# The row loop of a PEER layer: dot, weighting and sum of a row at three places of the order, four row buffers of their own, and four projections as steps between rows

## The chip, the cores and the metric

One NeuronCore of a Trainium2 chip runs the whole layer in one launch. The metric is the device time in microseconds; the kernel before took 913.14 us (median of 3 runs, 912.76 to 917.01). TensorE is called PE here, VectorE DVE, ScalarE ACT, GpSimd POOL, and SyncE SP, which only issues DMAs.

## The reference, cut to what matters

A decoder layer on x of 256 positions by 1024, in float32: normalised projections, two attention groups, an output product with residual, then a PEER layer, in which each position picks 128 of 16384 experts and adds their weighted rows.

```python
h = rms_norm(x, attn_norm); P = h @ w_in            # 1024 x 3072: six parts of 512 columns
mq, mk, mv, dq, dk, dv = split(P)                   # MoBA q k v, differential q k v
...
x = x + concat(A, B) @ w_out
xc = rms_norm(x, ffn_norm)
q  = (xc @ w_query).reshape(C, 8, 2, 128)
sc = einsum('thpd,hpnd->thpn', q, sub_keys)         # 8 heads x 2 x 128 keys
top_s, top_i = top_k(sc, 16)
cand_s = top_s[:, :, 0, :, None] + top_s[:, :, 1, None, :]
best_s, best_pos = top_k(cand_s.reshape(C, 8, 256), 16)
experts = take_along_axis(cand_i, best_pos); gates = softmax(best_s)
u, vv = expert_down[experts], expert_up[experts]    # 128 experts a position, 1024 + 1024 values each
act = gelu(einsum('cd,chkd->chk', xc, u))
x = x + einsum('chk,chkd->cd', gates * act, vv)
```

The output has the shape of x. Every position reads 128 rows of 8 KB, so 256 x 128 x 8 KB = 268 MB come out of HBM.

## The kernel before, in words

The positions are two halves of 128, A and B (`tt` 0 and 1), one position to a partition. First half A runs alone: six projections (`proj`, `evac`, `turn`), attention, output product, norm, and the first of its four routes. `route(tt, c4)` finds the experts of two of the eight heads: `query` (64 matmul instructions of 128 columns on PE), `keys`, then `route1` and `route2`, a chain on DVE with products on POOL. Each route makes 32 expert numbers (`eid`, L556). Then the six projections of half B run, and only behind them does the row loop begin.

A **slot** is one expert for 128 positions. `issue` (L579) starts a gather of 128 rows of 8 KB into a row buffer `uv` (1.05 MB, L586, on POOL's queue) as soon as a buffer is free and its number is known. `slots` (L591) then emits for that row, one after the other: the dot product on DVE (L599), Gelu, times gate, and the diagonal `dg` on ACT (L600, L601, L603), and the sum on PE (L607, four matmul instructions of 512 columns into `acc`), and gives the buffer back. There are 256 slots, 128 for each half. Between slots the loop takes steps of a generator `behind`: one a slot, and one more every fifth (1.2 a slot). The steps are A's three other routes, then `front` (attention, output product, residual and norm of half B), then B's four routes; `yield` marks where a step ends.

Behind `tc.manual_schedule()` (L695) the instructions stand on every engine in the order in which this loop emits them; ahead of it a scheduler interleaves the work. Each engine takes its queue strictly in order, so an instruction that waits holds up all that stand behind it. There are 9 row buffers (`RING1`), made from the memory that the projections give back, and 6 more (`RING2`) when `front` has ended. Weights come in tiles of 512 KB on SP's queue: 20 buffers `wts` for projections and output product, 4 buffers `wqp` for the queries. PSUM has 8 banks: 4 `psA`, and 4 `psB` that later become two for `acc` and two for B's output product. `hdot` has 3 buffers, so a fourth dot waits until ACT has used the first.

```python
while done[0] < NT * NSEL:
    slots(1)
    next(work, None)
    if done[0] % 5 == 0:
        next(work, None)
    issue()
```

Of the kernel before, what the change touches and what calls it, by code (L numbers as in the profile page):

```python
# [20 lines left out]
P = 128  # L21
T = 256
NT = 2
# [20 lines left out]

RING1 = 9
RING2 = 6
WRING = 20


@with_exitstack  # L50
def hymba_peer_kernel(ctx, tc, xT_d, x_d, an_d, fn_d, fnT_d, win_d, qkg_d, lam_d, og_d, wout_d,
# [19 lines left out]
    pw = pj.enter_context(tc.tile_pool(name="pw", bufs=2, side="right"))  # L71
    qop = pj.enter_context(tc.tile_pool(name="qop", bufs=3, side="right"))

# [99 lines left out]
    def proj(ci, tt):  # L173
        p = pps[ci, tt] = psB.tile([P, 512], FT, name="psB")
        for k in range(KC):
            PE.matmul(p, lhsT=xT[tt][:, k], rhs=W[ci + 6 * tt][k // 2][:, k % 2], start=(k == 0), stop=(k == KC - 1))  # L176

    def evac(ci, tt):
# [8 lines left out]
        sq = aw.tile([P, 8, HD], FT, name="sq")  # L187
        S.activation(sq.rearrange("p h d -> p (h d)"), p, AF.Square, scale=r1[tt])
        ss = small.tile([P, 8], FT, name="ssq")
        V.tensor_reduce(ss, sq, axis=AX.X, op=OP.add)  # L190
        rs = small.tile([P, 8], FT, name="rsq")
        rsqrt(rs, ss, 8, HD)
        g0, n = GRP[ci]
        nh = 8 // n
# [3 lines left out]
        for m in range(n):  # L198
            for hf in range(2):
                a = slice(hf * 32, hf * 32 + 32)  # L200
                b = slice(32 - hf * 32, 64 - hf * 32)
                G.tensor_tensor(tv[:, :, m, a], prv[:, :, m, b],  # L202
                                ropeS[tt][:, None, g0 + m, a].to_broadcast([P, nh, 32]), op=OP.mult)
            V.tensor_tensor(ov[:, :, m], prv[:, :, m],
                            ropeC[tt][:, None, g0 + m, :].to_broadcast([P, nh, HD]), op=OP.mult)
        G.tensor_tensor(o, o, t, op=OP.add)
        V.tensor_tensor(o, o, bc(rs, HD), op=OP.mult)
        pend[ci, tt] = o
# [188 lines left out]
    sk = rt1.tile([P, 2 * PH, NKEY], FT, name="sk")  # L397
    proj(2, A)
    evac(2, A)
    proj(3, A)  # L400
    evac(3, A)
    turn(2, A)
    proj(0, A)
    evac(0, A)
    turn(3, A)
    run(scores(A, MOBA))
    proj(1, A)
    turn(0, A)
    evac(1, A)
    lambdas()  # L410
    run(probsT(A, MOBA))
    proj(5, A)
    evac(5, A)
    run(attend(A, MOBA))
    turn(1, A)
    run(scores(A, DIFF))
    run(mixturn(A, MOBA))
    proj(4, A)
    evac(4, A)
    for q in range(4):  # L420
# [167 lines left out]

    acc = {}

    def slots(n):  # L591
        for _ in range(n):
            if done[0] == NT * NSEL:
                return
            tt, k = divmod(done[0], NSEL)
            uv = rows.pop(done[0])
            col = cols[done[0]]
            h = small.tile([P, 1], FT, name="hdot")
            V.scalar_tensor_tensor(uv[:, :D], uv[:, :D], 1.0, xn[tt], op0=OP.mult, op1=OP.mult, accum_out=h)  # L599
            S.activation(h, h, AF.Gelu)  # L600
            S.activation(h, h, AF.Copy, scale=gate[tt][:, col:col + 1])  # L601
            dg = diag.tile([P, P], FT, name="dg")
            S.activation(dg, ident, AF.Copy, scale=h)  # L603
            if k == 0:
                acc[tt] = psO.tile([P, 2, 512], FT, name="acc")
            for c in range(2):
                PE.matmul(acc[tt][:, c], lhsT=dg, rhs=uv[:, D + c * 512:D + (c + 1) * 512],  # L607
                          start=(k == 0), stop=(k == NSEL - 1))
            rings.append(home.pop(done[0]))
            done[0] += 1  # L610
            issue()
            if k == NSEL - 1:
                for c in range(2):
                    m = slice(c * 512, (c + 1) * 512)
                    V.tensor_tensor(x2[tt][:, m], acc[tt][:, c], x2[tt][:, m], op=OP.add)  # L615
                    nc.sync.dma_start(out_d[tt * P:(tt + 1) * P, m], x2[tt][:, m])

    load_q(0, wts)
    run(route(A, 0))


    for g in (2, 3, 0, 1, 5, 4):
        fetch(g + 6, win_d[g], wts)
    gain_x(B, slice(0, 4))
    gain_x(B, slice(4, 8))
    norm_in(B)
    tables(B)
    for g in (2, 3, 0, 1, 5, 4):
        proj(g, B)
        evac(g, B)  # L630
        if g in (3, 1):
            turn(g - 1, B)
            turn(g, B)
    pj.close()
    wst.close()
    psP.close()
    psO = ctx.enter_context(tc.tile_pool(name="psO", bufs=1, space=PSUM))
    psW = right.enter_context(tc.tile_pool(name="psW", bufs=2, space=PSUM))
    bs = ExitStack()
    bp["b"] = bs.enter_context(tc.tile_pool(name="bp", bufs=1, side="right"))  # L640
    wqp = ctx.enter_context(tc.tile_pool(name="wqp", bufs=4))
    xb = ctx.enter_context(tc.tile_pool(name="xb", bufs=1))
    lists(B, xb)
    diag = ctx.enter_context(tc.tile_pool(name="diag", bufs=3))
    rings += [ctx.enter_context(tc.tile_pool(name="gat1", bufs=RING1))] * RING1

    def front():

        yield from both(B, MOBA)
        yield from both(B, DIFF)  # L650
        bs.close()
        wo2 = right.enter_context(tc.tile_pool(name="wo2", bufs=4, side="right"))
        for n in range(2):
            fetch(("o", n, B), wout_d[n], wo2, (0, 1))
        yield
        for n in range(2):
            for k in range(4):
                wout(B, n, k, psW)
                yield
        for n in range(2):  # L660
            fetch(("o", n, B), wout_d[n], wo2, (2, 3))
        yield
        for n in range(2):
            for k in range(4, 8):
                wout(B, n, k, psW)
                yield
        yield from resid(B, xb)
        yield from norm(B, xb)
        right.close()
        rings.extend([ctx.enter_context(tc.tile_pool(name="gat2", bufs=RING2, side="right"))] * RING2)  # L670

    def behind():
        f = front()
        yield from route(A, 1, 2)
        for n, _ in enumerate(route(A, 2, 3)):
            yield
            if n % 2:
                next(f, None)
                yield
        for _ in route(A, 3):  # L680
            yield
            next(f, None)
            yield
        yield from f
# [4 lines left out]

    load_q(1, wqp)  # L690
    ctx.enter_context(tc.manual_schedule())
    issue()
    work = behind()
    while done[0] < NT * NSEL:
# [61 lines left out]
```

## Time and profile before

| | |
|---|---|
| median of 3 runs | 913.14 us |
| profiled execution, its time | 912.12 us |
| profiled execution, its span | 910.2 us |
| busy share of the span: PE, DVE, ACT, POOL | 80%, 54%, 34%, 43% |
| DMA | 323.14 MB, mean 355 GB/s |
| gathers (256) | 268.85 MB, 73.6% of the 16 DMA engines' span |

The span runs from the first to the last instruction; 1.9 us of the profiled time lie outside it. Matmuls are pipelined and their ends are modelled, so the busy share of PE is too high a figure for its work. The 40 slices of the page are 22.76 us each. The first gather starts at 147 us, the last lands at 901 us.

### The profile page before, as it was taken

Reading aid. Unit: us, or ns where it says so; the run is one execution under the profiler, and the core shown is the slowest. Engines: PE = TensorE matmul, PEld = TensorE weight load, DVE = VectorE, ACT = ScalarE, POOL = GpSimd, SP = SyncE. Lnnn points to the kernel's source line nnn. Section 1 sums busy time; section 2 is a strip of 40 time slices with the busy share of each in tenths; the row PEclk is TensorE's granted clock in tenths of the full one; section 3 lists DMA queues with packets and bytes.
Section 4 is the critical chain, followed back from the end, with each engine's and each line's share of the span. In section 5 each row is a group of like instructions: output and inputs, shape, how many; then the busy total and the mean of one; then the engine's idle time right before and its main releaser. Section 6 shows DMA issues by size and latency. Waiting matters only on the chain. (4 is left out here: it accounts for less than half of the span.)

```text
span 910.2 us, 8337 instructions
## 1 busy us (share of the span) xinstructions
PE 729.8 (80%) x2156; PEld 340.9 (37%) x2156; DVE 491.0 (54%) x1364; ACT 311.1 (34%) x936; POOL 395.4 (43%) x426
## 2 busy tenths in 40 slices
PE   6998796788777787699885768686999787788876
PEld 2555342545335432344533435342343222222222
DVE  4744761373763576463574463646774444555443
ACT  1421112242552355332333232323443333333332
POOL 3400434272272254333555372728355555555540
PEclk9999988999899998999998999999899999999999
DMA  9997507999879788999999998978899999999995
GB/s 354 408 404 250 185 0 269 417 422 382 319 292 376 278 310 351 339 370 421 391 415 420 419 370 303 355 244 354 350 422 419 422 421 419 421 422 420 422 420 224
DMA packets 52686, 323.14 MB, mean 355 GB/s; under 512 B 6240, under 2 KB 6496, under 8 KB 19744
## 3 DMA queue, kind: packets, MB, share of 16 engines
q0 software_dynamic: 36944, 268.85, 73.6%
q1 hardware_dynamic: 15264, 53.12, 15.3%
q10 hardware_dynamic: 432, 0.66, 0.2%
q8 instruction: 17, 0.28, 0.1%
q14 instruction: 29, 0.24, 0.1%
HBM read 321.55 MB, written 1.05 MB: 354 GB/s over the span
## 5 line engine op out<-in xcount | busy, mean ns | idle before, releaser
L607 PE MATMUL acc<-uv,dg 128*128 128x512 f32 x1024 | 510.3, 633 | 158.2 <-ACT dg L603 157.6
L586 POOL DMA_INDIRECT uv<-in_uv_dram,eid x256 | 298.4, 1166 | 390.1 <-PE acc L607 203.2
L599 DVE SCALAR_TENSOR_TENSOR uv<-uv,xn 128x1024 f32<-128x1024 f32 x256 | 309.4, 1221 | 176.6 <-DMA uv<-in_uv_dram,eid 143.1
L607 PEld LDWEIGHTS acc<-uv,dg 128*128 128x128 f32 x1024 | 186.6, 196 | 441.9 <-ACT dg L603 278.4
L600 ACT ACTIVATE hdot<-hdot 128x1 f32<-128x1 f32 x256 | 51.0, 199 | 300.3 <-DVE uv L599 300.1
L603 ACT ACTIVATE dg<-ident,hdot 128x128 f32<-128x128 f32 x256 | 102.8, 401 | 55.3 <-PE acc L607 48.2
L176 PE MATMUL psB<-w,xT 128*128 128x512 f32 x192 | 91.2, 628 | 6.9 <-DMA w<-in_win_dram 6.9
L601 ACT ACTIVATE hdot<-hdot,gate 128x1 f32<-128x1 f32 x256 | 75.3, 294 | 8.3
L460 PEld LDWEIGHTS psA<-xgT,w 128*128 128x128 f32 x512 | 63.9, 198 | 14.5 <-issue 14.2
L460 PE MATMUL psA<-xgT,w 128*128 128x128 f32 x512 | 63.6, 280 | 0.0
L495 DVE MAX8 tops<-sc 128x8 f32<-128x128 f32 x32 | 7.0, 280 | 92.2 <-ACT sc L474 92.2
L483 POOL TENSOR_TENSOR ci<-tf 128x4 f32<-128x4 f32 (+3 forms) x72 | 32.5, 481 | 55.1 <-DVE tf L511 55.0
L176 PEld LDWEIGHTS psB<-w,xT 128*128 128x128 f32 x192 | 37.3, 201 | 49.9 <-issue 47.4
L555 DVE TENSOR_REDUCE ef<-hit 128x16 f32<-128x320 f32 (+1 forms) x16 | 11.7, 735 | 45.0 <-POOL hit L541 45.0
L338 PE MATMUL psB<-w,mT 128*128 128x512 f32 x64 | 30.5, 594 | 0.7 <-ACT mT L329 0.7
L202 POOL TENSOR_TENSOR qt<-pr,rS 128x128 f32<-128x128 f32 (+1 forms) x24 | 14.8, 640 | 30.4 <-ACT pr L186 30.3
L464 ACT COPY qs<-psA 128x512 f32<-128x512 f32 x8 | 4.7, 585 | 65.1 <-PE psA L460 65.1
L541 POOL TENSOR_TENSOR hit<-hit,ci 128x160 f32<-128x160 f32 (+1 forms) x32 | 23.4, 766 | 0.9 <-DVE hit L538 0.8
L599 DVE DVE_READ_ACCUMULATOR uv<-uv,xn 128x1 f32 x256 | 20.8, 81 | 0.0
L338 PEld LDWEIGHTS psB<-w,mT 128*128 128x128 f32 x64 | 11.8, 190 | 14.3 <-issue 13.4
L186 ACT ACTIVATE pr<-psB,r 128x512 f32<-128x512 f32 x8 | 5.5, 687 | 33.4 <-PE psB L176 22.2
L245 DVE TENSOR_REDUCE mx<-psA 128x2 f32<-128x512 f32 (+1 forms) x12 | 8.1, 685 | 14.3 <-PE psA L240 14.3
(125 smaller groups left out, 407.4 us busy)
## 6 DMA issues: line engine op xcount, KB each, us to landing
w<-in_win_dram SPq DMA_DIRECT2D x48, 512.0 KB, 9.5
w<-in_wq_dram SPq DMA_DIRECT2D x28, 512.0 KB, 9.6
w<-in_wout_dram SPq DMA_DIRECT2D x16, 512.0 KB, 10.0
uv<-in_uv_dram,eid POOLq DMA_INDIRECT x256, 12.1
sk<-in_sk_dram SPq DMA_DIRECT2D x1, 1024.0 KB, 9.7
out_dram<-x SPq DMA_DIRECT2D x4, 256.0 KB, 3.5
xT<-in_xT_dram SPq DMA_DIRECT2D x2, 256.0 KB, 5.0
x<-in_x_dram ACTq DMA_DIRECT2D x1, 512.0 KB, 6.1
```

What stands on the lines that cost most here:

```text
L176: PE.matmul(p, lhsT=xT[tt][:, k], rhs=W[ci + 6 * tt][k // 2][:, k % 2], start=(k == 0), stop=(k == KC - 1))
L202: G.tensor_tensor(tv[:, :, m, a], prv[:, :, m, b], ropeS[tt][:, None, g0 + m, a].to_broadcast([P, nh, 32]), op=OP.mult)
L338: PE.matmul(wops[tt, n], lhsT=mixT[tt, MOBA if k < 4 else DIFF][:, k % 4], rhs=W["o", n, tt][k // 2][:, k % 2], start=(k == 0), stop=(k == ...
L460: PE.matmul(p[:, c], lhsT=w[k // 2][:, k % 2, c * P:(c + 1) * P], rhs=xgT[tt][:, k], start=(k == 0), stop=(k == KC - 1))
L483: eng.tensor_tensor(d, src[:, :, 1, b0:b0 + nb], src[:, :, 0, a0:a0 + 1].to_broadcast([P, 2, nb]), op=OP.add)
L541: G.tensor_tensor(e[:, h], e[:, h], ci[:, h, None, :n].to_broadcast([P, 8, n]), op=OP.mult)
L586: G.indirect_dma_start(out=rows[n], out_offset=None, in_=uv_d, in_offset=bass.IndirectOffsetOnAxis(ap=eid[tt][:, k:k + 1], axis=0))
L599: V.scalar_tensor_tensor(uv[:, :D], uv[:, :D], 1.0, xn[tt], op0=OP.mult, op1=OP.mult, accum_out=h)
L600: S.activation(h, h, AF.Gelu)
L601: S.activation(h, h, AF.Copy, scale=gate[tt][:, col:col + 1])
L603: S.activation(dg, ident, AF.Copy, scale=h)
L607: PE.matmul(acc[tt][:, c], lhsT=dg, rhs=uv[:, D + c * 512:D + (c + 1) * 512], start=(k == 0), stop=(k == NSEL - 1))
```

## The change

The four parts:

- **Slot in three places.** `slots` becomes `dot`, `weigh` and `add`. In the loop the sum of a slot always follows one slot later than before; once B's projections have ended (`lag[0] = 1`) the weighting too follows one slot later, and the sum two. `hdot` gets 6 buffers. A buffer is given back, and the next gather issued, by `add`.
- **Four row buffers of their own.** `gat0` (`RING0` = 4) has its memory from the start, so that gathers need not wait for the projections' memory. `RING1` falls from 9 to 5 and joins when B's projections have ended; `RING2` is as it was. To make room `WRING` falls from 20 to 8, `qop` from 3 to 2; the `wqp` pool is there from the start.
- **Four projections as steps.** Of B's six projections only 2 and 3 run ahead of the slots. The others (0, 1, 5, 4) are steps at the head of `front`, four steps for the matmuls of each and up to five for its evacuation; their weights are fetched when each begins. B's projections and output product share two `psB` banks.
- **1.45 steps a slot** in place of 1.2, with `front` beginning earlier among A's routes.

```diff
-RING1 = 9
+RING0 = 4
+RING1 = 5
 RING2 = 6
-WRING = 20
+WRING = 8
+STEPS = 1.45
...
-    psP = ExitStack()
-    psB = psP.enter_context(tc.tile_pool(name="psB", bufs=4, space=PSUM))
+    psB = ctx.enter_context(tc.tile_pool(name="psB", bufs=2, space=PSUM))
+    psO = ctx.enter_context(tc.tile_pool(name="psO", bufs=1, space=PSUM))
+    wqp = ctx.enter_context(tc.tile_pool(name="wqp", bufs=4))
+    diag = ctx.enter_context(tc.tile_pool(name="diag", bufs=3))
+    gat0 = ctx.enter_context(tc.tile_pool(name="gat0", bufs=RING0))
...
             PE.matmul(p, lhsT=xT[tt][:, k], rhs=W[ci + 6 * tt][k // 2][:, k % 2], start=(k == 0), stop=(k == KC - 1))
+            if k % 2:
+                yield
...
+    acc, lag, dots, ready_w = {}, [0], [], []
+
+    def dot():
+        n = done[0]
+        done[0] += 1
+        h = small.tile([P, 1], FT, name="hdot", bufs=6)
+        uv = rows[n]
+        V.scalar_tensor_tensor(uv[:, :D], uv[:, :D], 1.0, xn[n // NSEL], op0=OP.mult, op1=OP.mult, accum_out=h)
+        dots.append((n, h))
+
+    def weigh():
+        n, h = dots.pop(0)
...
+        S.activation(dg, ident, AF.Copy, scale=h)
+        ready_w.append((n, dg))
+
+    def add():
+        n, dg = ready_w.pop(0)
...
+        rings.append(home.pop(n))
+        issue()
...
     def slots(n):
         for _ in range(n):
...
+            dot()
+            last = done[0] == NT * NSEL
+            while len(dots) > (0 if last else lag[0]):
+                weigh()
+            while len(ready_w) > (0 if last else 1):
+                add()
...
+    def project(g):
+        fetch(g + 6, win_d[g], wts)
+        yield from proj(g, B)
+        yield from evac(g, B)
...
+    run(project(2), project(3))
+    rings += [gat0] * RING0
...
     def front():
 
+        for g in (0, 1, 5, 4):
+            yield from project(g)
+        pj.close()
+        wst.close()
...
+        rings.extend([ctx.enter_context(tc.tile_pool(name="gat1", bufs=RING1))] * RING1)
+        lag[0] = 1
         yield from both(B, MOBA)
...
+        yield from mix(route(A, 1, 2), f, 2, 1)
+        yield from mix(route(A, 2, 3), f, 1, 1)
+        yield from mix(route(A, 3), f, 1, 1)
...
+        while steps < STEPS * (done[0] + 1):
             next(work, None)
-        if done[0] % 5 == 0:
-            next(work, None)
+            steps += 1
```

POOL around the first gathers, before: `hit` are the products of A's first route, `qt` and `qo` belong to B's projections, `uv` is a row buffer.

```order
L541 TENSOR_TENSOR hit_780<-hit_780,ci 128x400 x2
L206 TENSOR_TENSOR qo<-qo,qt 128x512
L202 TENSOR_TENSOR qt<-pr,rS_861 128x8x32 x2
L206 TENSOR_TENSOR qo<-qo,qt 128x512
L202 TENSOR_TENSOR qt<-pr,rS_861 128x4x32 x4
L206 TENSOR_TENSOR qo<-qo,qt 128x512
L202 TENSOR_TENSOR qt<-pr,rS_861 128x4x32 x4
L206 TENSOR_TENSOR qo<-qo,qt 128x512
L586 DMA uv<-in_uv_dram,eid_659 128x2048 x19
L483 TENSOR_TENSOR ci<-tf 128x2x8
```

The same place in the changed kernel, up to the products of A's second route (`ci`):

```order
L553 TENSOR_TENSOR hit_800<-hit_800,ci 128x400 x2
L217 TENSOR_TENSOR qo<-qo,qt 128x512
L598 DMA uv<-in_uv_dram,eid_671 128x2048
L212 TENSOR_TENSOR qt<-pr,rS_833 128x8x32 x2
L598 DMA uv<-in_uv_dram,eid_671 128x2048
L217 TENSOR_TENSOR qo<-qo,qt 128x512
L598 DMA uv<-in_uv_dram,eid_671 128x2048 x11
L495 TENSOR_TENSOR ci<-tf 128x2x8
```

The first gather now stands behind the evacuation of B's first projection; before it stood behind the last POOL work of all six.

SP from A's first query weights on, before (`wq` query weights, `win` projection weights, `wout` output product; 512 KB each):

```order
L83 DMA w<-in_wq_dram 128x1024 x4
L83 DMA w<-in_win_dram 128x1024 x24
L83 DMA w<-in_wq_dram 128x1024 x12
L83 DMA w<-in_wout_dram 128x1024 x8
L83 DMA w<-in_wq_dram 128x1024 x12
L616 DMA out_dram<-x_93 128x512 x2
```

And now, from the same point on:

```order
L88 DMA w<-in_wq_dram 128x1024 x4
L88 DMA w<-in_win_dram 128x1024 x8
L88 DMA w<-in_wq_dram 128x1024 x4
L88 DMA w<-in_win_dram 128x1024 x4
L88 DMA w<-in_wq_dram 128x1024 x4
L88 DMA w<-in_win_dram 128x1024 x4
L88 DMA w<-in_wq_dram 128x1024 x4
L88 DMA w<-in_win_dram 128x1024 x8
L88 DMA w<-in_wout_dram 128x1024 x8
L88 DMA w<-in_wq_dram 128x1024 x12
```

Of the 24 projection tiles 8 stand ahead of the second query's weights; the other 16 are now interleaved with the query weights of A's routes.

PE in B's third route, before, over the last quarter of its query (`psA_3242` is the query's bank, `qs_3241` its copy in SBUF, `dg_` the diagonals of successive slots):

```order
L607 MATMUL acc_1131<-uv_2988,dg_3281 128x512 x2
L460 MATMUL psA_3242<-xgT1_2628,w_3045 128x128 x2
L460 MATMUL psA_3242<-xgT1_2628,w_3047 128x128 x2
L460 MATMUL psA_3242<-xgT1_2628,w_3049 128x128 x2
L460 MATMUL psA_3242<-xgT1_2628,w_3051 128x128 x2
L607 MATMUL acc_1131<-uv_3006,dg_3300 128x512 x2
L473 MATMUL psA_3315<-sk_195,qs_3241 128x128 x4
L607 MATMUL acc_1131<-uv_3024,dg_3325 128x512 x2
```

ACT at that place, before:

```order
L603 ACTIVATE dg_3281<-ident_105,hdot_3277 128x128
L464 COPY qs_3241<-psA_3242 128x512
L600 ACTIVATE hdot_3296<-hdot_3296 128x1
L601 ACTIVATE hdot_3296<-hdot_3296,gate0_660 128x1
L603 ACTIVATE dg_3300<-ident_105,hdot_3296 128x128
```

PE there now (`psA_3148` and `qs_3147` are the query's bank and copy):

```order
L472 MATMUL psA_3148<-xgT1_2595,w_2971 128x128 x2
L472 MATMUL psA_3148<-xgT1_2595,w_2973 128x128 x2
L472 MATMUL psA_3148<-xgT1_2595,w_2975 128x128 x2
L472 MATMUL psA_3148<-xgT1_2595,w_2977 128x128 x2
L627 MATMUL acc_994<-uv_2877,dg_3179 128x512 x2
L485 MATMUL psA_3221<-sk_207,qs_3147 128x128 x4
L627 MATMUL acc_994<-uv_2897,dg_3206 128x512 x2
```

And ACT there now:

```order
L617 ACTIVATE dg_3179<-ident_117,hdot_3157 128x128
L476 COPY qs_3147<-psA_3148 128x512
L614 ACTIVATE hdot_3175<-hdot_3175 128x1
L615 ACTIVATE hdot_3175<-hdot_3175,gate0_672 128x1
L617 ACTIVATE dg_3206<-ident_117,hdot_3175 128x128
```

Before, the sum right behind the query used the diagonal that stands on ACT behind the copy of that query (`dg_3300`). Now it uses one that stands ahead of the copy (`dg_3179`), and the one behind it (`dg_3206`) is used a sum later.

## Rows read from the trace of the kernel before

**Rows 1.** The page's span in 40 slices: granted TensorE clock and DMA in tenths, and GB/s.

```profile
PEclk9999988999899998999998999999899999999999
DMA  9997507999879788999999998978899999999995
GB/s 354 408 404 250 185 0 269 417 422 382 319 292 376 278 310 351 339 370 421 391 415 420 419 370 303 355 244 354 350 422 419 422 421 419 421 422 420 422 420 224
```

**Rows 2.** Busy time by stretch for line L599 alone, the dot product; the count holds two instructions for each slot. Columns: stretch, its length, DVE busy (count), granted clock, DMA share, GB/s.

```profile
147.00:303.00 156.00, 51.73 (x86) 0.92 0.91 358
303.00:432.00 129.00, 49.32 (x83) 0.96 0.92 352
432.00:495.00 63.00, 21.79 (x39) 0.95 1.00 408
495.00:637.00 142.00, 45.83 (x77) 0.94 0.88 344
637.00:680.00 43.00, 32.43 (x53) 0.90 0.94 384
680.00:901.40 221.40, 108.75 (x179) 1.00 1.00 415
```

**Rows 3.** Who waited for whom from 147 to 660 us: us in total, times, longest.

```profile
POOL uv L586 <- PE acc L607: 197.4, 80, 7.4
...
PE acc L607 <- ACT dg L603: 115.4, 64, 9.1
...
DVE tops L495 <- ACT sc L474: 86.5, 7, 15.9
ACT qs L464 <- PE psA L460: 58.9, 7, 11.0
DVE ef L555 <- POOL hit L541: 43.2, 12, 8.7
DVE uv L599 <- DMA uv<-in_uv_dram,eid: 33.3, 10, 17.0
```

**Rows 4.** The timeline of B's second route, from its first query step to the first maximum of its scores: start, us, engine, line, count, and in brackets the idle time before and what ended it.

```profile
543.53 3.78 PE L607 MATMUL acc<-uv,dg 128*128 128x512 f32 x4 [4.70 <-ACT dg L603]
...
551.89 1.88 PE L607 MATMUL acc<-uv,dg 128*128 128x512 f32 x4
...
555.59 0.58 ACT L464 COPY qs<-psA 128x512 f32<-128x512 f32 x1 [10.97 <-PE psA L460]
...
556.64 0.40 ACT L603 ACTIVATE dg<-ident,hdot 128x128 f32<-128x128 f32 x1
557.09 1.98 PE L607 MATMUL acc<-uv,dg 128*128 128x512 f32 x4 [1.54 <-ACT dg L603]
...
560.72 0.87 DVE L495 MAX8 tops<-sc 128x8 f32<-128x128 f32 x4 [14.81 <-ACT sc L474]
```

**Rows 5.** The timeline of the start of the slots: A's first route from its first maximum to its expert numbers, the end of the second projection's evacuation on DVE, the first gather, the first dot and its way to PE.

```profile
95.49 0.87 DVE L495 MAX8 tops<-sc 128x8 f32<-128x128 f32 x4 [5.61 <-ACT sc L474]
...
110.18 0.17 DVE L556 CAST eid<-ef 128x32 int32<-128x32 f32 x1
...
117.92 0.17 DVE L125 SCALAR_TENSOR_TENSOR rsq<-rs_a,rsq 128x8 f32<-128x8 f32 x1
...
147.35 1.03 POOL L586 DMA_INDIRECT uv<-in_uv_dram,eid  x1 [13.31 <-PE psB L176]
...
153.23 1.23 DVE L599 SCALAR_TENSOR_TENSOR uv<-uv,xn 128x1024 f32<-128x1024 f32 x1 [16.96 <-DMA uv<-in_uv_dram,eid]
...
154.50 0.20 ACT L600 ACTIVATE hdot<-hdot 128x1 f32<-128x1 f32 x1 [5.99 <-DVE uv L599]
...
155.56 3.78 PE L607 MATMUL acc<-uv,dg 128*128 128x512 f32 x4 [9.08 <-ACT dg L603]
```

**Rows 6.** The 256 gathers of line L586, from issue to landing.

```profile
DMA to landing us min/median/max: 5.4/12.1/24.2
```

**Rows 7.** The page's DMA queues (packets, MB, share of the 16 engines' span) and issues (count, KB each, us to landing): the gathers' queue and one kind of weight tile.

```profile
q0 software_dynamic: 36944, 268.85, 73.6%
...
w<-in_wq_dram SPq DMA_DIRECT2D x28, 512.0 KB, 9.6
```

**Rows 8.** PE's timeline: one query, the keys of one route, and a run of 20 projection matmuls of 512 columns.

```profile
85.44 7.46 PE L460 MATMUL psA<-xgT,w 128*128 128x128 f32 x64
...
93.60 1.14 PE L473 MATMUL psA<-sk,qs 128*128 128x128 f32 x8
...
120.97 8.75 PE L176 MATMUL psB<-w,xT 128*128 128x512 f32 x20
```

**Rows 9.** Busy time in one stretch of the instructions that write or read `psA` (queries, keys, transposes, attention). Columns: stretch, its length, busy of PE, PEld, DVE and ACT (count), clock, DMA share, GB/s.

```profile
303.00:660.00 357.00, 51.21 (x384) 47.47 (x376) 4.82 (x7) 11.88 (x29) 0.94 0.92 358
```

**Rows 10.** The same stretch for line L338, B's output product: busy of PE and PEld.

```profile
303.00:660.00 357.00, 16.02 (x32) 6.08 (x32) 0.94 0.92 358
```

**Rows 11.** The chain of waits at its end: two links of gathers eight slots apart, and two pieces behind the last landing.

```profile
721.59 19.13 DMA uv<-in_uv_dram,eid
...
741.50 19.07 DMA uv<-in_uv_dram,eid
...
901.40 1.24 DVE uv L599 x2
...
905.70 0.69 DVE x L615
```

More of the change, by code (lines that the diff above doesn't have):

```diff
@@ L397, in hymba_peer_kernel @@
     sk = rt1.tile([P, 2 * PH, NKEY], FT, name="sk")
[L398 to L401, printed above, removed]
+    run(proj(2, A))
+    run(evac(2, A))
+    run(proj(3, A))
+    run(evac(3, A))
     turn(2, A)
-    proj(0, A)
-    evac(0, A)
+    run(proj(0, A))
+    run(evac(0, A))
     turn(3, A)
     run(scores(A, MOBA))
-    proj(1, A)
+    run(proj(1, A))
     turn(0, A)
-    evac(1, A)
+    run(evac(1, A))
     lambdas()
     run(probsT(A, MOBA))
-    proj(5, A)
-    evac(5, A)
+    run(proj(5, A))
+    run(evac(5, A))
     run(attend(A, MOBA))
@@ L417, in hymba_peer_kernel @@
     run(mixturn(A, MOBA))
-    proj(4, A)
-    evac(4, A)
+    run(proj(4, A))
+    run(evac(4, A))
     for q in range(4):
@@ L587, in issue @@
                                  in_offset=bass.IndirectOffsetOnAxis(ap=eid[tt][:, k:k + 1], axis=0))
-    acc = {}
+    acc, lag, dots, ready_w = {}, [0], [], []
[8 more added lines that the diff above has]
+        n, h = dots.pop(0)
+        col = cols[n]
+        S.activation(h, h, AF.Gelu)
+        S.activation(h, h, AF.Copy, scale=gate[n // NSEL][:, col:col + 1])
+        dg = diag.tile([P, P], FT, name="dg")
+        S.activation(dg, ident, AF.Copy, scale=h)
+        ready_w.append((n, dg))
@@ new lines, in add @@
+    def add():
+        n, dg = ready_w.pop(0)
+        tt, k = divmod(n, NSEL)
+        uv = rows.pop(n)
+        if k == 0:
+            acc[tt] = psO.tile([P, 2, 512], FT, name="acc")
+        for c in range(2):
+            PE.matmul(acc[tt][:, c], lhsT=dg, rhs=uv[:, D + c * 512:D + (c + 1) * 512],
+                      start=(k == 0), stop=(k == NSEL - 1))
+        rings.append(home.pop(n))
+        issue()
+        if k == NSEL - 1:
+            for c in range(2):
+                m = slice(c * 512, (c + 1) * 512)
+                V.tensor_tensor(x2[tt][:, m], acc[tt][:, c], x2[tt][:, m], op=OP.add)
+                nc.sync.dma_start(out_d[tt * P:(tt + 1) * P, m], x2[tt][:, m])
@@ L591, in slots @@
     def slots(n):
         for _ in range(n):
[L593 to L623, printed above, removed]
+            dot()
[4 more added lines that the diff above has]
+                add()
+    load_q(0, wqp)
+    run(route(A, 0, 1))
     gain_x(B, slice(0, 4))
@@ L627, in hymba_peer_kernel @@
     tables(B)
-    for g in (2, 3, 0, 1, 5, 4):
-        proj(g, B)
-        evac(g, B)
+    ORDER_B = (2, 3, 0, 1, 5, 4)
+    def project(g):
+        fetch(g + 6, win_d[g], wts)
+        yield from proj(g, B)
+        yield from evac(g, B)
         if g in (3, 1):
             turn(g - 1, B)
+            yield
             turn(g, B)
[L634 to L645, printed above, removed]
-    def front():
+            yield
+    run(project(2), project(3))
+    rings += [gat0] * RING0
+    lists(B, const)
+    xb = []
+    def front():
+        for g in (0, 1, 5, 4):
+            yield from project(g)
+        pj.close()
+        wst.close()
+        bs = ExitStack()
+        bp["b"] = bs.enter_context(tc.tile_pool(name="bp", bufs=1, side="right"))
+        xb = ctx.enter_context(tc.tile_pool(name="xb", bufs=1))
+        rings.extend([ctx.enter_context(tc.tile_pool(name="gat1", bufs=RING1))] * RING1)
+        lag[0] = 1
         yield from both(B, MOBA)
@@ L652, in front @@
         wo2 = right.enter_context(tc.tile_pool(name="wo2", bufs=4, side="right"))
[L653 to L665, printed above, removed]
+        for q in (0, 2):
+            for n in range(2):
+                fetch(("o", n, B), wout_d[n], wo2, (q, q + 1))
+            yield
+            for k in range(2 * q, 2 * q + 4):
+                for n in range(2):
+                    wout(B, n, k, psB)
                 yield
@@ L670, in front, with mix @@
         rings.extend([ctx.enter_context(tc.tile_pool(name="gat2", bufs=RING2, side="right"))] * RING2)
+    def mix(r, f, nr, nf):
+        n = 0
+        for _ in r:
+            yield
+            n += 1
+            if n % nr == 0:
+                for _ in range(nf):
+                    next(f, None)
+                    yield
     def behind():
         f = front()
[L674 to L683, printed above, removed]
+        yield from mix(route(A, 1, 2), f, 2, 1)
+        yield from mix(route(A, 2, 3), f, 1, 1)
+        yield from mix(route(A, 3), f, 1, 1)
         yield from f
@@ L693, in hymba_peer_kernel @@
     work = behind()
+    steps = 0
     while done[0] < NT * NSEL:
         slots(1)
-        next(work, None)
-        if done[0] % 5 == 0:
+        while steps < STEPS * (done[0] + 1):
             next(work, None)
+            steps += 1
         issue()
```

8 lines of the change are left out of this document (6 added, 2 removed).

## The prediction

> **What bounds the kernel now.** I read the page's 40 slices first [rows 1]. Three stretches show: up to slice 6 the DMA runs for weights only and falls to nothing; the middle, from 147 to about 680 us, is uneven; from slice 31 on every slice but the last moves 419 to 422 GB/s. That last stretch is bounded by the DMA: on the chain of waits two gathers eight slots apart start at 721.59 and 741.50 [rows 11], so a row of 1.05 MB takes 19.91 / 8 = 2.49 us. Nothing in the change moves fewer rows, so time can be won only where the DMA does not run at this rate.
>
> Then the stretches, by the count of dots [rows 2] (two instructions for each slot). The DMA's mean over 147 to 680 is (156 x 358 + 129 x 352 + 63 x 408 + 142 x 344 + 43 x 384) / 533 = 361 GB/s, 86% of 421. It idles there for about 75 us in sum, and before 147 it carries no row at all. A slot takes (303 - 153.2) / 43 = 3.49 us in the first 43 slots, and (637 - 303) / 99.5 = 3.36 us in the next hundred.
>
> Who is late there [rows 3]: POOL waits 197 us to issue gathers because PE has not given a buffer back, while DVE waits only 33 us for rows. Rows lie ready and slots are slow. PE in turn waits 115 us for the diagonal, DVE 87 us for the scores of a route, ACT 59 us for queries. The timeline of B's second route [rows 4] shows how: ACT waits 10.97 us for PE's query to copy it, the next diagonal stands behind that copy, PE waits 1.54 us for the diagonal, and DVE 14.81 us for the scores. No engine is full; strict order couples them.
>
> **The start.** The first gather goes out at 147.35, and POOL waited for PE's `psB` ahead of it, the last projections [rows 5]. Its expert numbers exist at 110.18 + 0.17. With `gat0` it needs these and POOL's first evacuation only: 110.4, 37 us sooner. The first dot stands on DVE behind the second projection's evacuation (117.92 + 0.17), and 110.4 plus the 5.88 us that the first row took (147.35 to 153.23) is 116.3, so it comes at 118.1 in place of 153.2: 35 us. Fewer weight buffers and two `psB` banks ahead of it I cost at nothing: PE's projection tiles take 8.75 / 20 x 4 = 1.75 us each [rows 8], a tile lands in 9.6 us at the median [rows 7], and 8 tiles of lead are 14 us of PE; without that cover each late tile would cost up to 8 us.
>
> **First stage, 43 slots on four buffers.** The steps from here to the end of B's projections are 1.45 a slot. Four projections are 4 x 16 x 0.44 = 28 us of PE; about three queries add 22.4 and keys 2.3 [rows 8]. Lower bounds for a slot:
> - the loop of a buffer: dot 1.23, ACT 1.06 (154.50 to 155.56), sum 1.88, issue to first dot 5.88 [rows 4, 5]; 10.05 / 4 = 2.51 us. The fastest landing of all is 5.4, the median 12.1 [rows 6], but the median belongs to a full queue of 9 to 15 rows.
> - PE: sum 1.75, plus 53 / 43 = 1.23: 2.98 us.
> - DMA: 2.49, plus 20 weight tiles at 1.25 us (half a row each), 25 / 43 = 0.58: 3.07 us.
>
> So no less than 3.07. With nothing hidden the buffer's loop pays for the rest: 2.51 + 1.23 + 0.58 + 0.87, the last being DVE's chain of a route (95.49 to 110.35, 14.9 us, 2.5 routes over 43 slots): 5.2 us. The row nearest to it is the first 43 slots of before at 3.49, with the same dots and routes and nine buffers. I add the projections and weight tiles that are new there, (28 + 25) / 43 = 1.23, at three tenths, as they lie beside other engines' work: 3.85 us. 43 slots end at 118.1 + 165.6 = 284, before 303.
>
> **Second stage, slots 43 to 128.** Now nine buffers, later fifteen, and weighting and sum lag. Lower bounds: DMA 2.49 + 20 tiles x 1.25 / 85 = 2.78; PE 1.75 + (51 + 16) / 85 = 2.54 [rows 9, 10]. Before it was 3.36, 0.87 above the DMA's 2.49. The steps are 1.45 / 1.2 = 1.21 times as dense, which alone gives 3.36 + 0.21 x 0.87 = 3.54. Against it stands the lag: PE's 115 us for the diagonal, over some 157 slots, are 0.73 a slot. In the order the sum behind a query now uses a diagonal that stands on ACT ahead of the query's copy, so that wait goes there; ACT's and DVE's own waits for the query (59 and 87 us) do not, and they are late next. Between none and all of 0.73 I take two fifths, 0.29: 3.25 us. 85 slots take 276: slot 128 at 560, with B's last route found by then (1.45 steps a slot bring it there some 20 slots earlier than before).
>
> **Last stage.** From there nothing but rows: some 13 have landed ahead, so 115 x 2.49 = 286 us remain: last landing 846. The tail, from the last landing's dot (901.40) past the last write at 905.70 to the span's end at 910.2, is 9 us; two dots in it, as now: 855. With 1.9 outside the span 857; the median of the runs shown is 1.0 above the profiled 912.12, so 858. As a check: 141 rows and 21 MB of weights, 169 MB from 113 to 560, are 379 GB/s, 90% of 421, against 86% before.
>
> Edits at nothing: three more `hdot` buffers, the same instructions in another order; the last slot sheds its lag at once. A sum that comes one or two slots later holds its buffer 3 to 6 us longer; with four buffers this stands in the 3.85, with fifteen it is covered by the rows ahead.
>
> **The clock.** The granted clock is 0.92 in 147 to 303 and 1.00 from 680 [rows 2]. After 9.08 us idle PE's first sum took 3.78 us, after 4.70 again 3.78, and 1.88 eight us later [rows 4, 5]: these are its two levels, 1.2 and 2.4 GHz. Four buffers leave PE idle more often.
> The Trainium skill, page "TensorE: Matmul & The Clock Gate", section "Part 1: The HAM clock gate (the "warmup" mystery)", says that half rate is the default state and that only sustained activity releases it. The rows agree with both levels, and it speaks against four buffers; by that rule alone, with PE at half rate throughout the first stage, the forecast would become the slower rival below.
>
> **The rivals.**
> - *The bubbles stay.* The lag moves a wait from PE to ACT and DVE, and the DMA stays at 361 GB/s: 169.1 MB / 0.361 = 468 us, slot 128 at 581, then 286 + 9 + 2 + 1: 879. For it: 87 us of DVE waiting for scores and 43 for `hit` [rows 3] are not touched. Against: the denser steps end sooner. It covers 868 to 905.
> - *The DMA is nearly full from the first gather.* At 97% of 421, 169.1 MB take 414 us: slot 128 at 527, the end at 825. The floor, all 290 MB at 421 from 113, is 689 + 113 + 11 = 813. For it: 0.73 us a slot of PE waits; against: the 3.07 of the first stage leaves no slack on four buffers.
> - *The gain is eaten.* Rows start 37 us sooner but the four buffers take 4.8 us a slot (43 slots: 206 us, 41 more than forecast): 858 + 41 and up, 899 to 917.
> - *Slower: four buffers and a slow PE.* A sum of 3.78 stands in the buffer's loop, and the loop becomes serial with PE's steps: (10.05 + 1.9) / 4 = 2.99 in place of 2.51, and queries and projections at half rate are 2 x 53 / 43 = 2.47 in place of 1.23; with 0.58 and 0.87 that is 6.9 if nothing overlaps, and 2 x 2.98 = 5.96 if PE alone decides. At 6.0 slot 43 comes at 376, 92 us later than forecast: 950. It decides from 3.85 + 56 / 43 = 5.15 us a slot on. For it: the 3.78 at the start, and PE, ACT and DVE waiting in turn even with nine buffers. Against: a clock of 0.92 with the same kind of waits, and four projections that give PE long runs of work.
>
> **How the numbers follow.** A measurement of this kernel can tell about 0.5% from no change: below 908.6 is faster, above 917.7 slower. Forecast 858 (its own range 835 to 868) 0.46; bubbles stay 0.24; DMA nearly full 0.11; gain eaten 0.08, of which a part ends within 0.5%; slower 0.11. Faster is then 0.46 + 0.24 + 0.11 + 0.01 = 0.82, the same 0.07, slower 0.11. The range leaves out at its low end half of the DMA-bound case, above it the last two: 826 to 908. The ends of the unknown costs give it too: 3.07 a slot in the first stage and 2.78 in the second would be 118 + 132 + 236 + 298 = 784, less than the floor, so 813 stands; 5.2 and 3.54 give 118 + 224 + 301 + 298 = 941.
>
> **What would show it.** First gather at 110 and first dot at 118. Slot 43 at 284, with 350 GB/s till then, slot 128 at 560, and 421 GB/s from there. PE's wait for the diagonal falls from 115 us to below half; the waits of DVE for scores stay. I am wrong if the first 43 slots take over 5.15 us each, with DVE waiting for rows and a clock well under 0.92, or if the diagonal's wait goes and the DMA still moves 361 GB/s up to slot 128.

## The result and the profile after

The changed kernel took 879.49 us (median of 4 runs, 873.64 to 882.52) against 912.95 us for the kernel before (4 runs, one more than above): ratio 0.962, 95% interval 0.956 to 0.968. The profiled execution took 878.93 us, its span 877.2 us. The prediction was 858, its range 826 to 908.

The page's 40 slices, now of 21.93 us each, with the rows that answer to [rows 1]:

```profile
PEclk9999969999999899988999999999999999999999
DMA  9969559989997999996999999999999999999993
GB/s 352 350 200 363 204 194 381 382 295 390 418 343 263 396 386 421 349 344 241 344 417 417 418 418 419 420 420 420 421 419 420 421 418 420 421 420 421 420 419 153
```

Counted from 1, rows now move from slice 6 on, and every slice from 21 (439 us) to 39 moves 417 GB/s and more, where before this began with slice 30 (660 us). In between lie four weak places: slices 6, 9, 12 to 13, and 17 to 20 with 241 GB/s at the bottom.

Busy time by stretch for the dots' line, L608, as in [rows 2]: stretch, its length, DVE busy (count, two instructions for each slot), granted clock, DMA share, GB/s.

```profile
113.00:284.00 171.00, 57.74 (x90) 0.95 0.89 339
284.00:395.00 111.00, 45.75 (x72) 0.92 0.97 379
395.00:425.00 30.00, 3.67 (x6) 0.89 0.72 247
425.00:560.00 135.00, 53.24 (x88) 0.96 1.01 415
560.00:581.00 21.00, 15.05 (x26) 0.92 1.01 421
581.00:868.00 287.00, 140.65 (x228) 1.00 0.99 411
```

Against 421 GB/s the DMA loses 171 x (1 - 339/421) = 33 us in the first stage, 11 in the next stretch, 12 in the 30 us behind 395, where only three dots run, and 2 in the 135 us up to 560: 59 us, most of it in the first stage, on four buffers.

Who waited for whom from 110 to 600 us, as in [rows 3]: us in total, times, longest.

```profile
POOL uv L598 <- PE acc L627: 181.5, 71, 10.9
...
DVE uv L608 <- DMA uv<-in_uv_dram,eid: 72.8, 43, 3.8
PE acc L627 <- ACT dg L617: 50.6, 33, 3.9
...
ACT qs L476 <- PE psA L472: 26.9, 6, 10.0
DVE x L358 <- PE psB L350: 26.0, 2, 25.8
DVE ef L567 <- POOL hit L553: 25.8, 9, 6.7
DVE tops L507 <- ACT sc L486: 25.0, 6, 12.7
```

Not only PE's wait for the diagonal has fallen (115 to 51); ACT's for a query (59 to 27) and DVE's for scores (87 to 25) fell with it. Two waits are new or larger: DVE for rows (33 to 73), and once 25.8 us for the output product.

The timeline of B's second route now, from its query's copy to the first maximum of its scores, the place of [rows 4]:

```profile
501.27 0.56 ACT L476 COPY qs<-psA 128x512 f32<-128x512 f32 x1
501.41 2.87 PE L627 MATMUL acc<-uv,dg 128*128 128x512 f32 x4 [2.02 <-ACT dg L617]
...
504.08 1.88 PE L485 MATMUL psA<-sk,qs 128*128 128x128 f32 x8
505.78 6.79 PE L627 MATMUL acc<-uv,dg 128*128 128x512 f32 x15
505.99 0.69 ACT L486 ACTIVATE sc<-psA,r 128x512 f32<-128x512 f32 x1 [3.29 <-PE psA L485]
...
506.71 0.87 DVE L507 MAX8 tops<-sc 128x8 f32<-128x128 f32 x4 [2.91 <-ACT sc L486]
```

Here the copy has waited for nothing (10.97 us before) and DVE 2.91 us for the scores (14.81 before); behind the keys PE runs at least 15 matmuls of sums in one piece, so their diagonals come in time. Other queries still wait: the 26.9 us of ACT above are six waits.

Starts of dots in the traces of this study (us; each the first instruction of that dot on DVE), used below:

```
dot            0      43     128    255
before         153.2  303.3  595.6  901.4
changed        118.7  279.2  563.6  868.3
e1 undone      118.4  284.7  650.9  946.0
e2 spread      155.8  288.1  539.2  849.8
e3 wout        118.6  281.7  549.6  854.6
e4 1.2 steps   117.5  276.0  543.8  864.2
e5 lag early   117.4  289.2  573.0  875.6
e6 five        119.5  270.4  552.3  857.3
e7 weigh       118.3  279.2  577.1  875.7
e8 wout+five   117.8  270.3  544.4  849.7
e9 sum         155.5  285.3  536.3  844.6
e10 1.2 undone 117.7  277.2  600.4  927.7
e11 copies     152.0  278.8  559.5  868.1
e12 wout+six   124.6  271.2  536.2  841.5
```

### The profile page after: what moved, and what is told of

Its sections match the earlier page's. It is cut to its first block, busy times and chain, and to the rows that moved or that the text cites. A ratio compares the mean times of both kernels' runs of the same rounds, so it can differ in the third digit from the quotient of the medians.

```text
span 877.2 us, 8338 instructions
## 1 busy us (share of the span) xinstructions
PE 725.2 (83%) x2156; PEld 337.4 (38%) x2156; DVE 497.9 (57%) x1364; ACT 311.8 (36%) x936; POOL 401.1 (46%) x426
## 4 chain that ended last, share of the span: by engine, by line
DMA 47%; PE 33%; DVE 9%; issue 5%; ACT 3%; POOL 2%; SPq 0%; DVEq 0%; POOLq 0%; ACTq 0%
DMA uv<-in_uv_dram,eid 43%; PE acc L627 14%; PE psB L181 7%; PE psA L472 4%; DVE uv L608 3%; DMA w<-in_wout_dram 3%; PE psB L350 3%; PE psA L252 1%; POOL hit L553 1%; PE psA L301 1%; POOL uv L598 1%; DMA w<-in_win_dram 1%; PE psA L485 1%; PE psA L251 1%; ACT dg L617 1%
## 5 line engine op out<-in xcount | busy, mean ns | idle before, releaser
L598 POOL DMA_INDIRECT uv<-in_uv_dram,eid x256 | 319.7, 1249 | 362.9 <-PE acc L627 182.6
L608 DVE SCALAR_TENSOR_TENSOR uv<-uv,xn 128x1024 f32<-128x1024 f32 x256 | 315.5, 1243 | 220.6 <-DMA uv<-in_uv_dram,eid 210.5
L627 PEld LDWEIGHTS acc<-uv,dg 128*128 128x128 f32 x1024 | 183.1, 194 | 395.5 <-ACT dg L617 235.5
L495 POOL TENSOR_TENSOR ci<-tf 128x4 f32<-128x4 f32 (+3 forms) x72 | 22.6, 344 | 56.8 <-DVE tf L523 56.7
L350 PE MATMUL psB<-w,mT 128*128 128x512 f32 x64 | 32.3, 640 | 8.3 <-DMA w<-in_wout_dram 7.6
L553 POOL TENSOR_TENSOR hit<-hit,ci 128x160 f32<-128x160 f32 (+1 forms) x32 | 25.8, 838 | 0.9 <-DVE hit L550 0.7
L358 DVE TENSOR_TENSOR x<-psB,x 128x512 f32<-128x512 f32 x4 | 2.8, 691 | 33.9 <-PE psB L350 33.9
L608 DVE DVE_READ_ACCUMULATOR uv<-uv,xn 128x1 f32 x256 | 21.4, 83 | 0.0
L226 PE MATMUL psA<-ident,qo 128*128 128x128 f32 x32 | 5.8, 311 | 12.4 <-DVE qo L219 12.4
```

Source lines behind the costliest of these rows:

```text
L350: PE.matmul(wops[tt, n], lhsT=mixT[tt, MOBA if k < 4 else DIFF][:, k % 4], rhs=W["o", n, tt][k // 2][:, k % 2], start=(k == 0), stop=(k == ...
L495: eng.tensor_tensor(d, src[:, :, 1, b0:b0 + nb], src[:, :, 0, a0:a0 + 1].to_broadcast([P, 2, nb]), op=OP.add)
L553: G.tensor_tensor(e[:, h], e[:, h], ci[:, h, None, :n].to_broadcast([P, 8, n]), op=OP.mult)
L598: G.indirect_dma_start(out=rows[n], out_offset=None, in_=uv_d, in_offset=bass.IndirectOffsetOnAxis(ap=eid[tt][:, k:k + 1], axis=0))
L608: V.scalar_tensor_tensor(uv[:, :D], uv[:, :D], 1.0, xn[n // NSEL], op0=OP.mult, op1=OP.mult, accum_out=h)
```

## The experiments

Theory 1 was the prediction's: the gain is the head start, the spread trims some idle time. Rival A: the spread carries the gain. Rival B: it costs, by holding buffers.

**e1, the spread undone.** In the changed kernel:

```diff
-            while len(ready_w) > (0 if last else 1):
+            while len(ready_w) > 0:
...
-        lag[0] = 1
```

> The changed kernel with dot, weighting and sum of a slot in one place again, rest as changed. Theory 1 (the gain is the head start of 35 us; the spread only trims the idle time of the DMA in the row loop, which is about 65 us in the changed kernel against 73 before): 5 to 12 us slower than the changed kernel, 884 to 892 us, with PE's wait for the diagonal back from 51 to 80 us or more between 110 and 600 us. Rival A (the spread carries the gain: without it four buffers take over 5 us a slot): 905 us or more. Rival B (the spread holds each of the four buffers a slot longer and costs time in the first stage): 876 us or less, and slot 43 before 270 us.

965.45 us, ratio to before 1.058 (1.052 to 1.065): 86 us slower than the changed kernel and slower than before. Theory 1 falls. But A's condition does not hold either: the first 43 slots took (284.7 - 118.4) / 43 = 3.87 us, not over 5. The loss lies behind them, (650.9 - 284.7) / 85 = 4.31 us a slot (its trace is of a run of 956.74 us, the shortest of its four). Its waits from 284 to 660 us show the same set as before:

```profile
POOL uv L598 <- PE acc L627: 179.6, 54, 8.5
...
PE acc L627 <- ACT dg L617: 90.5, 51, 6.4
DVE tops L507 <- ACT sc L486: 64.9, 5, 14.9
...
ACT qs L476 <- PE psA L472: 50.5, 5, 10.8
```

**e2, the spread alone.** The kernel before with `dot`, `weigh`, `add` called by `slots`, `lag[0] = 1` from the start, and six `hdot` buffers as in the changed kernel:

```diff
-    acc = {}
+    acc, lag, dots, ready_w = {}, [1], [], []
...
+        h = small.tile([P, 1], FT, name="hdot", bufs=6)
...
+            dot()
+            last = done[0] == NT * NSEL
+            while len(dots) > (0 if last else lag[0]):
+                weigh()
+            while len(ready_w) > (0 if last else 1):
+                add()
```

> The kernel before with the spread slot alone (weighting one slot later and sum two, from the first slot on; 9 buffers, all six projections ahead). Theory 1: 5 to 10 us faster than before, 903 to 908 us; PE's wait for the diagonal under 60 us where it was 115. Rival A: 895 us or less. Rival B: 913 us or more.

856.54 us, ratio 0.935 (0.929 to 0.942). Rival A holds: the spread alone wins 55 us, though its first gather leaves at 150. The rest of the change, put on top, costs 23 us.

**e3, the output product as before.** The changed kernel with the loops of the kernel before: the two column halves `n` one after the other, and a `yield` behind each `wout`. The changed kernel has `n` inside and one `yield` for both halves of a `k`.

```diff
-            for k in range(2 * q, 2 * q + 4):
-                for n in range(2):
-                    wout(B, n, k, psB)
+        for n in range(2):
+            for k in range(4):
+                wout(B, n, k, psB)
+                yield
...
```

> The changed kernel with the output product of half B in 18 steps as in the kernel before, in place of 4. Theory 1: the hole of the DMA at 395 to 425 us (247 GB/s, 12 us lost) comes of the four dense steps, in which DVE's residual stands ahead of the dots while PE waits for weight tiles: without it 867 to 873 us, and DVE's wait for that product falls from 26 us to below 10. Rival: the step count decides, 14 more steps put B's routes 10 slots later and give the gain back: 876 to 884 us.

866.71 us, ratio 0.950 (0.945 to 0.955): 13 us, at the low edge of what was expected. The product takes 10 steps in the changed kernel, not the 4 that the text above says: two that fetch, and eight with one `k` of both halves; e3 makes them 18. DVE's wait:

```profile
DVE x L358 <- PE psB L350: 6.7, 1, 6.7
```

The changed kernel's timeline shows what the denser steps did: PE waits for a weight tile of the second half, and DVE, whose residual is emitted behind the last of these steps, 25.84 us for PE; all later dots stand behind it.

```profile
404.22 2.08 PE L350 MATMUL psB<-w,mT 128*128 128x512 f32 x2 [5.35 <-DMA w<-in_wout_dram]
...
416.07 0.69 DVE L358 TENSOR_TENSOR x<-psB,x 128x512 f32<-128x512 f32 x1 [25.84 <-PE psB L350]
```

In e3 PE waits for no tile of this product. Step count and loop order were changed together; which of them won the 13 us is not shown.

**e4, 1.2 steps a slot** (`STEPS = 1.2`).

> The changed kernel at 1.2 steps a slot. Theory 1: B's last route ends some 25 slots later, the DMA reaches its 420 GB/s later, but each slot on the way is faster: 884 to 892 us. Rival (idle time goes by the step, not by the slot): 877 to 882 us, the same. Rival (dense steps overload the slots with four buffers): 872 us or less.

880.41 us, ratio 0.964 (0.959 to 0.969): the same as the changed kernel; the rival holds. With the spread in, the density of the steps is worth nothing: dot 128 comes 20 us sooner, and the 127 slots behind it take 16 us longer (320 against 305).

Theory 2: four buffers pace the first stage. Rival C: weights and PE do.

**e5, the weighting's lag from the first slot on.**

```diff
-    acc, lag, dots, ready_w = {}, [0], [], []
+    acc, lag, dots, ready_w = {}, [1], [], []
```

> The changed kernel with the weighting one slot late and the sum two from the first slot on, not from the end of half B's projections. Theory 2 (four buffers pace the first stage: about 15 us from one dot on a buffer to the next, 11 of them from issue to dot, 3.73 us a slot; a later sum lengthens that loop by a slot): slot 43 at 310 to 325 us where it was at 279, the whole 890 to 905 us. Rival A (the spread pays wherever it stands, as in the spread alone, 3.08 us a slot in the first 43 slots): slot 43 at 255 to 270 us, the whole 858 to 870 us.

887.7 us, ratio 0.976 (0.972 to 0.980), 8 us slower, slot 43 at 289. The sign is theory 2's, the size below what it said (slot 43 is 10 us later, not 31 to 46): both values lie between the two stated ranges.

**e6, five own buffers.**

```diff
-RING0 = 4
-RING1 = 5
+RING0 = 5
+RING1 = 4
...
-WRING = 8
+WRING = 6
```

> The changed kernel with five row buffers of their own and four that join in place of 4 and 5, and 6 weight buffers in place of 8 to make the room. Theory 2: a loop of 15 us over five buffers is 3.0 to 3.2 us a slot, slot 43 at 250 to 260 us, and the whole 858 to 866 us, if the first stage's 20 us are kept to the end. Rival C (late weights and PE's steps pace the first stage, not the buffers; two weight buffers fewer make that worse): slot 43 at 278 us or later, 878 us or more.

867.48 us, ratio 0.953 (0.949 to 0.957), 12 us faster. The whole came 1.5 us and slot 43 (270) 10 us later than theory 2 allowed: 3.51 us a slot in place of 3.73. DVE's wait for rows up to slot 43, in the changed kernel (113 to 284 us) and here (113 to 270):

```profile
DVE uv L608 <- DMA uv<-in_uv_dram,eid: 55.2, 31, 3.8
```

```profile
DVE uv L608 <- DMA uv<-in_uv_dram,eid: 35.3, 23, 3.7
```

So buffers are a part of what paces this stage, by 0.22 us a slot, not all of it.

**e7, the weighting never late.**

```diff
-        lag[0] = 1
```

> The changed kernel with the sum one slot late throughout and the weighting never late: one of the two halves of the spread undone. If the weighting's lag carries the 86 us that the spread is worth in the changed kernel (ACT does it ahead of the copy of a query it would stand behind): 930 to 955 us, PE's wait for the diagonal between 284 and 585 us over 60 us where it is 23. If the sum's lag carries it: 880 to 895 us. If each gives its share: 900 to 925 us.

883.95 us, ratio 0.971 (0.966 to 0.976): some 4 of the 86 us, within what a repeat differs by. PE's wait for the diagonal between 284 and 585 us is 36 us, not over 60 (23 in the changed kernel). In the changed kernel the sum's single slot carries the spread.

**e8, output product as before and five own buffers** (the edits of e3 and e6).

> Two edits in one: five own buffers (and 6 weight buffers) and the output product of half B in 18 steps. Theory 2: the two holes are apart in time, so the gains add: 12 of the output product and 15 to 20 of the buffers, 844 to 853 us, below the spread alone (856.5). Rival (what one gives back the other takes, since the DMA cannot be moved past its 420 GB/s: both end at the same bound): 860 to 868 us.

854.68 us, ratio 0.937 (0.931 to 0.943). The gains add (13 + 12 = 25); the upper end of the range was missed by 2 us, and the time is level with e2, not below it.

Theory 3: the sum's slot works because PE no longer stands at a diagonal that ACT makes behind the copy of PE's own query. Rivals D to F stand in the texts.

**e9, the sum's lag alone.** e2 with `lag = [0]`: on the kernel before, the sum one slot late, and the six `hdot` buffers of e2, which the text does not name.

> The kernel before with the sum one slot late throughout and nothing else (weighting at once, 1.2 steps, 9 buffers). Theory 3 (the sum's one slot carries nearly all of the spread, because PE no longer stands at a diagonal that ACT makes behind the copy of the query PE has just ended): 856 to 866 us, against 856.5 for the whole spread alone and 912 for before; PE's wait for the diagonal between 150 and 600 us at 60 us or less where it was 103. Rival D (with nine buffers and the projections ahead it takes both lags): 875 to 895 us.

855.39 us, ratio 0.935 (0.931 to 0.939), the same as e2 and half a microsecond below theory 3's range. The waits of the kernel before from 150 to 600 us:

```profile
POOL uv L586 <- PE acc L607: 180.6, 74, 7.4
...
PE acc L607 <- ACT dg L603: 103.2, 57, 9.1
...
DVE tops L495 <- ACT sc L474: 77.9, 6, 15.9
ACT qs L464 <- PE psA L460: 52.6, 6, 11.0
...
DVE uv L599 <- ACT dg L603: 20.1, 9, 5.1
```

And in e9, whose routes end sooner, from 150 to 550 us:

```profile
POOL uv L586 <- PE acc L615: 129.6, 68, 5.8
...
DVE tops L495 <- ACT sc L474: 53.2, 7, 10.3
...
PE acc L615 <- ACT dg L605: 52.1, 32, 13.8
...
ACT qs L464 <- PE psA L460: 33.9, 6, 7.5
...
DVE uv L596 <- ACT dg L605: 3.7, 2, 2.4
```

PE's wait for the diagonal up to 600 us is 58.4, within the 60 that were expected. The last row is dots that wait until ACT frees an `hdot` buffer: 20.1 us before, 3.7 here. What six buffers alone are worth was not run; e1 has six and no lag, and is slower than before. The clock does not explain the gain: the granted clock from 284 to 560 us was 0.95 before and is 0.96 in e9.

Its GB/s in 40 slices, of 21.3 us: with nine buffers and a late start the DMA is close to full from slice 9 on, but for slice 12.

```profile
GB/s 349 408 410 268 264 8 98 348 419 419 417 339 401 419 392 408 418 418 420 418 419 418 418 419 419 419 419 417 422 417 420 420 420 420 420 421 419 421 420 135
```

**e10, the spread undone at 1.2 steps** (the edits of e1 and e4).

> The changed kernel with the spread undone (965 us) and at 1.2 steps a slot. Theory 3: without the spread each step costs its whole round trip over PE, ACT and DVE, so a slot takes longer the denser the steps (4.31 us a slot between 43 and 128 at 1.45 steps), while the number of steps to be done stays: 955 to 972 us, slots 43 to 128 at 3.9 us or less, and the end of the steps some 25 slots later. Rival E (dense steps are what costs; at 1.2 the coupling is that of before): 915 to 940 us.

938.56 us, ratio 1.026 (1.023 to 1.030): rival E's range. Slots 43 to 128 took (600.4 - 277.2) / 85 = 3.80 us where 1.45 steps took 4.31; that sign is theory 3's, but the whole lies well below its 955 to 972. Without the spread dense steps cost 27 us; with it nothing (e4).

**e11, copies a step later.** The kernel before, slot in one place:

```diff
+        yield
         S.copy(q, p)
         qs[tt, c4] = q
...
+        yield
         S.activation(sc.rearrange("p a b -> p (a b)"), p.rearrange("p a b -> p (a b)"), AF.Copy, scale=r2[tt])
```

> The kernel before with one edit that leaves the slot in one place: ACT's copy of a query and of a route's scores is emitted one step later, so that the weighting of the next slot stands ahead of it on ACT. Theory 3: PE no longer waits for a diagonal behind its own query, which is what the sum's lag gives too, but the attention's steps stay coupled: 875 to 895 us, with PE's wait for the diagonal below 75 us. Rival F (DVE's steps, and not ACT's copies, hold the dots and so the diagonals): 905 to 915 us, the same as before.

881.2 us, ratio 0.965 (0.961 to 0.969). Two `yield` win 32 us, where the sum's lag wins 58 (e9): a later place for the two copies is worth over half of it, although each route has two steps more. Its first 43 slots take (278.8 - 152.0) / 43 = 2.95 us, as few as in e9 (3.02), and the next 85 take 3.30, where e9 takes 2.95. The waits from 150 to 570 us: DVE's for scores falls furthest, PE's for the diagonal to 80, not below 75, and ACT's for a query not at all (52.6 before).

```profile
PE acc L609 <- ACT dg L605: 80.1, 49, 8.9
ACT qs L465 <- PE psA L460: 54.0, 6, 11.0
...
DVE tops L497 <- ACT sc L476: 33.0, 4, 13.7
```

**e12, output product as before and six own buffers** (`RING0 = 6`, `RING1 = 3`, `WRING = 4`).

> The output product of half B in 18 steps, and six own buffers, three that join, and 4 weight buffers. Theory 2 (buffers pace the first stage): slot 43 at 262 us or sooner where it was 270 with five, and 845 to 852 us. Rival C (weights pace it now: 4 buffers hold one projection): first dot after 121 us or slot 43 at 272 or later, 856 us or more.

850.99 us, ratio 0.931 (0.928 to 0.934): the time is theory 2's, the signs are mixed. With 4 weight buffers the first dot is 6 us late (124.6), rival C's sign, and slot 43 comes at 271, not at 262 or sooner; counted from the first dot, 43 slots take 147 us where five buffers took 152.5 (e8). It is the fastest kernel here, though its interval overlaps those of e2, e8 and e9, and e9 is the kernel before with its slot alone rewritten.

## Why the prediction was right and wrong

The time lay in the range and the direction was right. The reasons were half wrong: in the second stage two errors covered each other, and that its sum came out is luck. Of the signs that the prediction named, one failed (DVE's waits for scores did not stay), and its sign of being wrong was nearly met: the diagonal's wait fell by more than half, and up to 560 us the DMA moved 366 GB/s, hardly more than the 361.

**The start: right.** First gather at 111.14 (forecast 110.4), first dot at 118.66 (118.1).

**First stage: right in size.** (279.2 - 118.7) / 43 = 3.73 us (3.85), slot 43 at 279 (284), with 339 GB/s (350). That four buffers hurt was right in sign (e6). The clock stayed up: 0.95 from 113 to 284, so PE did not run at half rate there. (The Trainium skill, page "TensorE: Matmul & The Clock Gate", section "Part 1: The HAM clock gate (the "warmup" mystery)", has half rate as the default that activity releases; a granted 0.95 in this stretch says that four buffers left activity enough.) The slower rival's condition, 5.15 us a slot, was not met even with the spread undone (3.87).

**Second stage: the step that failed.** Slots 43 to 128 took 3.35 us, forecast 3.25, and look right. Both terms were wrong. "The steps are 1.45 / 1.2 = 1.21 times as dense, which alone gives 3.36 + 0.21 x 0.87 = 3.54": without the spread it is 4.31 (e1), 0.77 more. Denser steps cost 0.51 a slot there, not 0.18 (4.31 against 3.80 in e10): 0.33 of the 0.77. The other 0.44 are there at 1.2 steps too (3.80 against 3.36 before), so they come of the rest of the change. One cause, at least with the spread in, is an edit whose cost I never worked out, the output product in 10 steps in place of 18: 0.20 us a slot (e3: (549.6 - 281.7) / 85 = 3.15). Against it "two fifths, 0.29" for the lag: it is 4.31 - 3.35 = 0.96. A part of this may be PE's rate, since the granted clock from 284 to 560 us is 0.91 in e1 and 0.94 in the changed kernel; it was not separated.

The sentence that failed is "ACT's and DVE's own waits for the query (59 and 87 us) do not [go], and they are late next". They went, to 27 and 25, and in e9 one edit at the sum takes all three rows down (103 to 52, 53 to 34, 78 to 53). So they were not three separate causes, as I read them in [rows 3]. My reading of why is one loop: the query's matmuls and keys themselves stand on PE behind a sum that waits for ACT, so one late diagonal is counted at three engines in turn. That is argued, not shown, and it is not the whole: in e11 PE's row falls by 23 us and DVE's by 45, ACT's stays, and the time still falls by 32.

**Last stage: mis-sized.** (868.3 - 563.6) = 305 us remained at slot 128 where 286 were forecast. That "some 13 have landed ahead" was too many: by 563 us the gathers' queue had moved 144.02 MB, which is 137 rows, 9 ahead; four rows are 10 us. The check in the forecast assumed 379 GB/s from 113 to 560; the stretches give (171 x 339 + 111 x 379 + 30 x 247 + 135 x 415) / 447 = 366, 6 MB less by then. The other 9 us are the end: 119 rows at 2.49 us from 563.6 on would be 860, and up to there (564 to 860) the DMA did move 420 GB/s, but the last row could be used only at 868 (last section). The tail was 9 us as forecast; its "two dots" are the two instructions of one dot, which changes nothing in the sum.

**The rivals.** "The bubbles stay" said 361 GB/s and 879 us, and the time was 879. Its rate was nearly met (366), but not for its reason: the coupling's waits fell by more than half, and the DMA idled at new places, on four buffers and at the output product, which are 33 and 12 of its 59 us.

**What the parts are worth.** Sum one slot later, and six `hdot` buffers with it: 58 us on the kernel before (e9). Weighting one slot later: nothing that can be told from no change (e2 beside e9, e7). The early start with four buffers and projections between slots: with e3's and e6's edits the whole takes 854.68, level with the spread alone. The earlier start is given back: e8 begins 38 us before e9, but its first 43 slots take 3.55 us, in e9 (285.3 - 155.5) / 43 = 3.02, and the next 85 take 3.23 against 2.95, about 23 us in each stage. That a part of the first is projection tiles, 12 x 1.25 = 15 us of DMA time now inside the row loop (of the 16 that were moved, four go out at 94 to 100 us, ahead of the first gather), is worked out and was not run by itself. What costs the second stage its 23 us is open.

## What to carry to other kernels

Where in-order engines hand work round (PE, ACT, PE), waits at several engines need not be separate causes: look at what each waiting instruction stands behind before giving each row a price of its own. Emit the consumer one round later; try this one edit alone before moving other work under it, since here it won 58 us and the rest gave back 24 of them. Where steps are merged in an emission order, look at the next instruction of another engine that is emitted behind them: DVE's residual held the dots behind it for 26 us.

## What had not been expected of the hardware

At the end of the changed kernel the DMA is nearly done some 6 us before the last row can be used. The stretches there, in the columns of the first windows:

```profile
855.00:860.00 5.00, 2.47 (x4) 1.00 1.02 419
860.00:862.00 2.00, 1.14 (x1) 1.00 0.68 274
862.00:864.00 2.00, 0.75 (x3) 1.00 0.22 90
864.00:866.00 2.00, 0.73 (x3) 1.00 0.07 29
866.00:868.00 2.00, 1.08 (x2) 1.00 0.05 20
```

The mean over 16 DMA engines falls to 0.22 behind 862 while dots go on one by one up to 868. In the kernel before the same fall begins behind 896, and the last dot starts at 901.4. A share of 0.07 or 0.05 of 16 engines is about one engine (1.1 and 0.8). So one engine seems to run behind the others at the end, and each row waits for its last piece; which, and why more so now, the trace does not tell, and it was not tried.

The chain of waits shows a second thing. In the last stage of the changed kernel its links are eight rows long, and most take 19.14 to 19.17 us, but three take 1 us more:

```profile
606.75 19.15 DMA uv<-in_uv_dram,eid
626.70 20.13 DMA uv<-in_uv_dram,eid
...
727.42 20.13 DMA uv<-in_uv_dram,eid
...
828.14 20.14 DMA uv<-in_uv_dram,eid
```

They lie 101 us apart. With them a row takes (868.3 - 583.6) / 113 = 2.52 us, not 2.49. In e9 such links start at 603.00, 723.66 and 824.39. What causes them is not known.
